# Last two tiles of tokens summed in PSUM: seeds from ScalarE, and a final norm that reads PSUM by halves

## The chip, the cores and the metric

The kernel runs on one core of a Trainium2 chip. A core has five engines, each with an instruction queue of its own: TensorE (PE in the profile, with its weight loads as PEld), VectorE (DVE), ScalarE (ACT), GpSimd (POOL) and SyncE (SP), which here issues nearly all the DMAs. PSUM, where TensorE's products land, has eight banks of 128 partitions x 512 float32 values; ScalarE and VectorE read and write it, too. The metric is the device time of one execution in microseconds (us); less is better.

## The reference, cut to what matters

One decoder layer for 512 tokens of 1024 channels: two kinds of attention, a residual, a mixture of 32 experts (each token goes to two of them), a second residual, and a last RMSNorm. What matters here is the end:

```python
x = x + hierarchical_moe(rmsnorm(x, ffn_norm[l]), ...)     # out[slot_tok] += ys * slot_w
return rmsnorm(x, final_norm)                              # x * rsqrt(mean(x*x) + eps) * final_norm
```

So the output of a token needs the sum of its residual row and of all its experts' rows, then the sum of squares over its 1024 channels, then one scaling of the row by a factor of its own and by the norm's gains.

## The kernel before, in words

The 512 tokens stand in four tiles of 128 tokens, `self.x2[0]` to `self.x2[3]`, each 128 partitions x 1024 float32 in SBUF. The experts are worked through in 16 pairs (`experts`, q = 0 to 15). A pair takes 64 slots of tokens for each of its two experts, so 128 rows. Its steps are: gate and up products into the PSUM tiles `G` and `U` (`gate_up`, L778), SiLU on ACT (L783) and a product on DVE (L784), a transposition of the result (`act_T`: L790 on PE, a copy on ACT, L792), the down products by halves of 512 channels (`down_products`, L804, tile `yp`), and a split of each half into a high and a low float32r part, scaled by the slot's weight (`down_split`: L811 on ACT, then L812 on DVE).

For most pairs the rows come back to their tokens by a product with a one-hot matrix `S` (`combine`): for each half and each of the four tiles two matmuls (high part L824, low part L825) write a PSUM tile `cp`, and VectorE adds it to `x2[t]` (L826). That makes 8 combines, 16 matmuls and 8 additions a pair. They are not done in their own pair: the list `todo` carries them into the next one, where PE takes five after the gate and up products and three after the transposition. Five pairs (`VIA`) go through DRAM instead; what they gathered is added to a tile by `take_slots` and L914, the last of it in pair 14, to `x2[3]`.

PSUM at that stage: `G` and `U` one bank each (pool `gp`), two banks for `yp` (pool `yp`, tag "y"), four for `cp` and the transpositions (pool `mp2`, tag "m").

The last pair ends in `last`. There PE computes both halves of the down products, then combines: half 0 of tile 0, and from there half 0 of the next tile and half 1 of this one in turn. As soon as a tile is whole, `final_factor` squares it with a sum on ACT (L965, which takes an instruction that reads the accumulator, and L966, which adds epsilon), `final_power` raises the sum to -1/2 on POOL (L969), and `final_scale` multiplies tile, factor and gains on DVE (L976) and issues the DMA to the output on SP (L977; tile 3 in two halves). Tile 0 goes another way: POOL multiplies it by the gains early (L946, into `o`), and ACT scales it by its factor (L952, DMA L953).

The order on PE and POOL is that of the program over all of `experts`; in `last` that holds for DVE and ACT as well. Everywhere else, and on SP always, the framework's planner sets the order by its own estimates of time. After `last` comes `overflow`: every engine loads a count (L995) and branches (L996) around a block that runs only if an expert has more than 64 tokens; the inputs here don't enter it.

Of the kernel before, what the change touches and what calls it, by code (L numbers as in the profile page):

```python
# [10 lines left out]
F32 = mybir.dt.float32  # L11
# [5 lines left out]
AF = mybir.ActivationFunctionType  # L17
ALU = mybir.AluOpType
# [3 lines left out]
P = 128  # L22
T = 512
NT = T // P
# [12 lines left out]
class Layer:  # L37
# [757 lines left out]
    def down(self, wd, aT, sw, half):  # L795
        return self.down_split(self.down_products(wd, aT, half), sw, half)

    def down_products(self, wd, aT, half):
        nc = self.nc
        yp = self.yp.tile([P, 512], F32, name="yp", tag="y")  # L800
        for j in range(2):
            for e in range(2):
                es = slice(64 * e, 64 * e + 64)
                nc.tensor.matmul(yp[es], aT[:, j, es], wd[e][:, j * D + half * 512:j * D + half * 512 + 512],  # L804
                                 start=j == 0, stop=j == 1)
        return yp
# [10 lines left out]
        self.nc.vector.tensor_scalar(S, self.tm, xf, None, ALU.is_equal)  # L817
        return S

    def combine(self, S, y, half, t):  # L820
        nc = self.nc
        hs = slice(half * 512, half * 512 + 512)
        cp = self.mp.tile([P, 512], F32, name="cp", tag="m")
        nc.tensor.matmul(cp, S[:, t * P:(t + 1) * P], y[0], start=True, stop=False)  # L824
        nc.tensor.matmul(cp, S[:, t * P:(t + 1) * P], y[1], start=False, stop=True)  # L825
        nc.vector.tensor_tensor(self.x2[t][:, hs], self.x2[t][:, hs], cp, ALU.add)  # L826

    def slot_rows(self):

# [32 lines left out]
    def experts(self):  # L862
        nc, tc = self.nc, self.tc
        NP = NE // 2
        wgu, wd = {}, {}
        for q in range(3):
            wgu[q], wd[q] = self.load_gu(q), self.load_d(q)
        self.yhl = self.wp.tile([P, 2048], F32R, name="yhl", tag="whi")
        with tc.manual_schedule(engines={mybir.EngineType.PE, mybir.EngineType.Pool}):
            xT, sw, xg = {0: self.xT0}, {}, {}  # L870
            S, y, todo, taken = None, None, [], []
            for q in range(NP):
                if q > 0 and q + 2 < NP:
                    wgu[q + 2], wd[q + 2] = self.load_gu(q + 2), self.load_d(q + 2)
                    if q + 2 == NP - 1:
                        self.load_final()
                r = wg[:, NE:NE + 1] if q else None

                def some(n):
                    for _ in range(min(n, len(todo))):  # L880
                        self.combine(S, y[todo[0][0]], *todo[0])
                        todo.pop(0)

                def between(j):
                    if q == 0 and j == 3:
                        self.tokens()
                        xg[1] = self.gather_rows(self.xi[:, 1:2], self.rows)
                    if q == 0 and j == 5:
                        sw[0] = self.take_weights()
                    if q == 0 and j == 9:  # L890
                        self.count_blocks()
                a = self.gate_up(wgu.pop(q), xT.pop(q), lambda: r if q else sw[0][1], between)
                def next_rows():
                    xT[q + 1] = self.new_xT()
                    for g in range(2):
                        self.gathered_T(xg[q + 1][0], xT[q + 1], g)
                if q == 0:
                    next_rows()
                n = min(len(todo), 4) if VIA[0] <= q <= VIA[-1] + 1 else len(todo)
                some((n + 1) // 2 + (n > 4))  # L900
                aT = self.act_T(*a)
                if q:
                    sw[q] = [self.slot_weights(q, wg, nc.scalar.copy)[:, 0:1]]
                some(n // 2 - (n > 4))
                if 0 < q < NP - 1:
                    next_rows()
                if q + 1 < NP:
                    wg = xg.pop(q + 1)[1]
                if q + 2 < NP:
                    xg[q + 2] = self.gather_rows(self.xi[:, q + 2:q + 3])  # L910
                if q == 1:
                    self.slot_rows()
                for t, r in taken:
                    nc.vector.tensor_tensor(self.x2[t], self.x2[t], r, ALU.add)  # L914
                t = q - VIA[-1] - 1
                taken = [self.take_slots(t, i) for i in range(2)] if 0 <= t < NT else []
                dn = wd.pop(q)
                if q in VIA:
                    self.down_out(dn, aT, sw[q][0], q)
                    continue  # L920
                S = self.one_hot(self.xf[:, q:q + 1])
                y = [None, None]
                todo = [(h, t) for h in range(2) for t in range(NT)]
                if q == NP - 1:
                    self.last(S, dn, aT, sw[q][0])
                    break
                for h in range(2):
                    y[h] = self.down(dn, aT, sw[q][0], h)

    def last(self, S, dn, aT, sw):  # L930

        nc, E = self.nc, mybir.EngineType
        self.out = [self.big.tile([P, 2, D], F32, name="fin", tag="big") for _ in range(2)]
        with self.tc.manual_schedule(engines={E.DVE, E.Activation}):
            nc.scalar.mul(self.fin[:, 0], self.fin[:, 0], D ** 0.5)
            yp = [self.down_products(dn, aT, h) for h in range(2)]
            y = [self.down_split(yp[0], sw, 0), None]
            self.combine(S, y[0], 0, 0)
            y[1] = self.down_split(yp[1], sw, 1)
            for t in range(NT):  # L940
                if t + 1 < NT:
                    self.combine(S, y[0], 0, t + 1)
                self.combine(S, y[1], 1, t)
                if t == 0:
                    o = self.out[0][:, 0]
                    nc.gpsimd.tensor_tensor(o, self.x2[0], self.fin[:, 0], ALU.mult)  # L946
                self.final_factor(t)
                if t:
                    self.final_power(t)
                if t == NT - 2:  # L950
                    self.final_power(0)
            nc.scalar.mul(o, o, self.rf[0])  # L952
            nc.sync.dma_start(self.io["out"][0, 0:P, :], o)  # L953
            for t in range(1, NT):
                self.final_scale(t, 2 if t == NT - 1 else 1)

    def load_final(self):
        nc = self.nc
# [92 lines left out]
    def run(self):  # L1051
        tc, ctx = self.tc, self.ctx
        self.oT = [None, None]
        self.nw, self.loads, self.rf = 0, [], {}
        PS = dict(space=PSUM, reuse_waits="tile")
        SB = dict(reuse_waits="tile")
        ctx.enter_context(tc.tile_pool(name="edge", bufs=1, side="right")).tile([P, 24], F32, name="pad")
        self.wp = ctx.enter_context(tc.tile_pool(name="wp", bufs=2, side="right", **SB))
        with ExitStack() as a:
            self.acc = a.enter_context(tc.tile_pool(name="acc", bufs=4, **PS))  # L1060
            self.mp = a.enter_context(tc.tile_pool(name="mp", bufs=3, **PS))
            self.op = a.enter_context(tc.tile_pool(name="op", bufs=1, **PS))
            with tc.tile_pool(name="rw", bufs=2, side="left", **SB) as self.rw:
                self.normed_T()
                self.load_consts()
                self.mla_compress()
                self.route_setup()
                self.mla_qkv()
                self.attention(0, range(4))
                self.moba_qkv()  # L1070
                self.attention(1, range(4))
            self.bl = ctx.enter_context(tc.tile_pool(name="bl", bufs=3, side="left", **SB))
            Ga = self.gate_T(CC + 1536)
            Gb = self.gate_T(CC + 2560)
            self.mix(Ga, Gb)
            self.attn_out()
        self.gp = ctx.enter_context(tc.tile_pool(name="gp", bufs=1, **PS))
        self.yp = ctx.enter_context(tc.tile_pool(name="yp", bufs=2, **PS))
        self.mp = ctx.enter_context(tc.tile_pool(name="mp2", bufs=4, **PS))
        self.experts()  # L1080
        self.overflow()
# [186 lines left out]
```

## Time and profile before

| | |
|---|---|
| time, median of 3 runs | 682.37 us (682.04 to 683.69) |
| the profiled execution | 683.7 us, of it span 681.9 us |
| PE busy | 661.3 us (97% of the span) |
| DVE, ACT, POOL busy | 376.1, 283.3, 83.3 us |
| chain that ended last | PE 92%, DVE 4%, ACT 1%, DMA 1% |

The span runs from the first to the last instruction that the profiler saw; the 1.8 us between span and time lie around it. L12 is line 12 of the kernel. A row of the timeline gives start, duration, engine, line, operation, the tiles (out<-in), how many, and in brackets how long the engine had been idle and what ended it. Names with a q at their end (SPq, POOLq) are an engine's sequencer: it loads registers, branches and issues DMAs.

### The profile page before, as it was taken

Reading aid. Unit: us, or ns where it says so; the run is one execution under the profiler, and the core shown is the slowest. Engines: PE = TensorE matmul, PEld = TensorE weight load, DVE = VectorE, ACT = ScalarE, POOL = GpSimd, SP = SyncE. Lnnn points to the kernel's source line nnn. Section 1 sums busy time; section 2 is a strip of 40 time slices with the busy share of each in tenths; the row PEclk is TensorE's granted clock in tenths of the full one; section 3 lists DMA queues with packets and bytes.
Section 4 is the critical chain, followed back from the end, with each engine's and each line's share of the span. In section 5 each row is a group of like instructions: output and inputs, shape, how many; then the busy total and the mean of one; then the engine's idle time right before and its main releaser. Section 6 shows DMA issues by size and latency. Waiting matters only on the chain.

```text
span 681.9 us, 11080 instructions
## 1 busy us (share of the span) xinstructions
PE 661.3 (97%) x4182; PEld 508.6 (75%) x4182; DVE 376.1 (55%) x944; ACT 283.3 (42%) x653; POOL 83.3 (12%) x127
## 2 busy tenths in 40 slices
PE   7999999999999999999999999999999999999991
PEld 7998887777788888888888899755666566666651
DVE  4624957877847983533568224643234332566654
ACT  4737545654639673433334153322222222222223
POOL 0604000000000000000000001212111111334303
PEclk8999999999999999999999999999999999999996
DMA  7733442101073026221398948799999999999953
GB/s 254 128 103 66 86 163 73 62 1 62 15 200 96 1 63 185 68 87 62 137 331 306 392 169 287 256 408 408 409 415 416 410 410 414 415 412 416 413 194 125
DMA packets 75656, 152.06 MB, mean 223 GB/s; under 512 B 31860, under 2 KB 54476, under 8 KB 63824
## 3 DMA queue, kind: packets, MB, share of 16 engines
q1 hardware_dynamic: 67616, 138.70, 55.9%
q0 software_dynamic: 4944, 8.35, 3.6%
q10 hardware_dynamic: 3040, 4.27, 2.4%
q8 instruction: 34, 0.56, 0.3%
q14 instruction: 22, 0.18, 0.1%
HBM read 149.57 MB, written 6.88 MB: 229 GB/s over the span
## 4 chain that ended last, share of the span: by engine, by line
PE 92%; DVE 4%; ACT 1%; DMA 1%; issue 1%; POOL 0%; SPq 0%; POOLq 0%; DVEq 0%
PE yp L804 8%; PE G L778 8%; PE U L778 8%; PE pacc L97 5%; PE pacc L96 5%; PE pacc L95 5%; PE pacc L451 4%; PE pacc L449 4%; PE pacc L450 4%; PE cp L824 3%; PE ptr L422 3%; PE cp L825 3%; PE S L404 3%; PE O L430 2%; PE pacc L493 2%; PE pacc L494 2%
## 5 line engine op out<-in xcount | busy, mean ns | idle before, releaser
L66 DVE SCALAR_TENSOR_TENSOR wlo<-wraw,ms,whi 128x256 fp32r<-128x256 f32 (+2 forms) x134 | 68.3, 551 | 31.1 <-ACT whi L65 30.9
L65 ACT ACTIVATE whi<-wraw,ms 128x256 fp32r<-128x256 f32 (+2 forms) x134 | 67.0, 560 | 42.1 <-PE pacc L450 19.8
L95 PE MATMUL pacc<-whi,hThi 128*128 128x352 f32 (+1 forms) x192 | 73.0, 380 | 0.0
L96 PE MATMUL pacc<-wlo,hThi 128*128 128x352 f32 (+1 forms) x192 | 70.4, 368 | 0.0
L97 PE MATMUL pacc<-whi,hTlo 128*128 128x352 f32 (+1 forms) x192 | 70.4, 366 | 0.0
L784 DVE SCALAR_TENSOR_TENSOR a<-U,wg,a 128x256 f32<-128x256 f32 x15 | 10.3, 686 | 101.8 <-issue 68.9
L804 PE MATMUL yp<-w,a 128*64 128x512 f32 x256 | 58.5, 598 | 0.5 <-ACT a L792 0.5
L778 PE MATMUL G<-w,xT 128*64 128x256 f32 x512 | 58.3, 380 | 0.0
L778 PE MATMUL U<-w,xT 128*64 128x256 f32 x512 | 58.2, 379 | 0.0
L778 PEld LDWEIGHTS G<-w,xT 128*64 128x64 f32 x512 | 36.5, 137 | 24.6 <-issue 4.9
L826 DVE TENSOR_TENSOR x<-x,cp 128x512 f32<-128x512 f32 x88 | 54.2, 682 | 0.8 <-PE cp L825 0.8
L778 PEld LDWEIGHTS U<-w,xT 128*64 128x64 f32 x512 | 36.7, 137 | 18.4
L449 PE MATMUL pacc<-hThi,whi 128*128 128x512 f32 x128 | 50.4, 393 | 0.0
L451 PE MATMUL pacc<-hThi,wlo 128*128 128x512 f32 x128 | 50.3, 393 | 0.0
L450 PE MATMUL pacc<-hTlo,whi 128*128 128x512 f32 x128 | 49.9, 390 | 0.0
L417 ACT ACTIVATE E<-E,mx 128x128 f32<-128x128 f32 (+3 forms) x64 | 35.6, 558 | 20.4 <-DVE mx L414 19.6
L1107 POOL TENSOR_SCALAR sq<-sq 128x1 f32<-128x1 f32 x4 | 0.9, 220 | 343.4 <-ACT junk L1104 343.4
L95 PEld LDWEIGHTS pacc<-whi,hThi 128*128 128x128 f32 x192 | 36.5, 190 | 4.9 <-issue 1.4
L96 PEld LDWEIGHTS pacc<-wlo,hThi 128*128 128x128 f32 x192 | 36.6, 191 | 4.2 <-issue 0.7
L804 PEld LDWEIGHTS yp<-w,a 128*64 128x64 f32 x256 | 17.0, 136 | 30.2 <-issue 27.8
L97 PEld LDWEIGHTS pacc<-whi,hTlo 128*128 128x128 f32 x192 | 36.4, 189 | 3.9 <-issue 0.2
L824 PE MATMUL cp<-yhl,S 128*128 128x512 f32 x88 | 37.6, 427 | 0.0
(232 smaller groups left out, 1338.8 us busy)
## 6 DMA issues: line engine op xcount, KB each, us to landing
w<-in_w_exp_gate_dram SPq DMA_DIRECT2D x32, 1024.0 KB
w<-in_w_exp_up_dram SPq DMA_DIRECT2D x32, 1024.0 KB
w<-in_w_exp_down_dram SPq DMA_DIRECT2D x30, 1024.0 KB
wraw<-in_w_in_dram SPq DMA_DIRECT2D x14, 1024.0 KB
wraw<-in_w_out_dram SPq DMA_DIRECT2D x4, 1024.0 KB
wraw<-in_w_in_dram SPq DMA_DIRECT2D x5, 704.0 KB
yd<-y POOLq DMA_DIRECT2D x5, 512.0 KB, 8.5
xs<-in_x_dram SPq DMA_DIRECT2D x4, 512.0 KB
```

Of the source, the lines that this page charges most:

```text
L65: nc.scalar.mul(hi[:, k], raw[:, k], g)
L66: nc.vector.scalar_tensor_tensor(lo[:, k], raw[:, k], g, hi[:, k].bitcast(F32), ALU.mult, ALU.subtract)
L95: nc.tensor.matmul(ps[t][:, :ncols], act_hi[kk // 4][:, kk % 4, ts], hi[:, k], start=kk == 0, stop=False)
L96: nc.tensor.matmul(ps[t][:, :ncols], act_hi[kk // 4][:, kk % 4, ts], lo[:, k], start=False, stop=False)
L97: nc.tensor.matmul(ps[t][:, :ncols], act_lo[kk // 4][:, kk % 4, ts], hi[:, k], start=False, stop=kk == ktot - 1)
L449: nc.tensor.matmul(ps, hi[:, k, ds], self.hT[0][k // 4][:, k % 4], start=k == 0, stop=False)
L450: nc.tensor.matmul(ps, hi[:, k, ds], self.hT[1][k // 4][:, k % 4], start=False, stop=False)
L451: nc.tensor.matmul(ps, lo[:, k, ds], self.hT[0][k // 4][:, k % 4], start=False, stop=k == KD - 1)
L778: nc.tensor.matmul(GU[i][es, 0:256], xT[:, j, es], gu[e][i][:, j * 256:(j + 1) * 256], start=j == 0, stop=j == KD - 1)
L804: nc.tensor.matmul(yp[es], aT[:, j, es], wd[e][:, j * D + half * 512:j * D + half * 512 + 512], start=j == 0, stop=j == 1)
L824: nc.tensor.matmul(cp, S[:, t * P:(t + 1) * P], y[0], start=True, stop=False)
L826: nc.vector.tensor_tensor(self.x2[t][:, hs], self.x2[t][:, hs], cp, ALU.add)
```

## The change

The last pair starts with `seed`: ScalarE copies the four halves of tiles 2 and 3 from SBUF into PSUM, tile 2 into two of the four "m" banks, tile 3 into both "y" banks. From there on `combine` for these tiles adds its two matmuls onto the seeded bank and does no VectorE addition; this holds for pair 14's products (which are combined during pair 15, in the order of tiles 0, 2, 1, 3) and for pair 15's. As the "y" banks are taken, pair 15's down products go to the two "m" banks left, and half 0 of tiles 1 and 0 in `last` to the banks of `G` and `U`.

In `last` the order becomes: half 0 of tiles 2, 3, 1, 0, then half 1 of tiles 2, 3, 1, 0. `final_part` squares half a tile straight from PSUM and adds epsilon or the first half's sum. Tiles 2 and 3 are scaled first, by halves from PSUM, and leave in one DMA each; tile 1 is scaled from SBUF in two halves; tile 0 keeps its way over POOL and ACT. POOL's order is the factors of tiles 2 and 3, the multiplication for tile 0, the factors of tiles 1 and 0. At the end ACT copies the four halves back from PSUM to `x2`, for `overflow`.

```diff
-    def down_products(self, wd, aT, half):
+    def down_products(self, wd, aT, half, at=None):
         nc = self.nc
-        yp = self.yp.tile([P, 512], F32, name="yp", tag="y")
+        pool, tag = at or (self.yp, "y")
+        yp = pool.tile([P, 512], F32, name="yp", tag=tag)
...
-    def combine(self, S, y, half, t):
+    def combine(self, S, y, half, t, at=None):
...
+        sums = self.sums.get((half, t))
+        if sums is not None:
+            for yi in y:
+                nc.tensor.matmul(sums, S[:, t * P:(t + 1) * P], yi, start=False, stop=yi is y[1], skip_group_check=True)
+            return
...
+    def seed(self):
+
+        for t, pool, tag in ((NT - 2, self.mp, "m"), (NT - 1, self.yp, "y")):
+            for h in range(2):
+                self.sums[h, t] = ps = pool.tile([P, 512], F32, name="sum", tag=tag)
+                self.nc.scalar.copy(ps, self.x2[t][:, h * 512:h * 512 + 512])
...
+                if q == NP - 1:
+                    self.seed()
+                    todo = [(h, t) for t in (0, 2, 1, 3) for h in range(2)]
...
-            yp = [self.down_products(dn, aT, h) for h in range(2)]
-            y = [self.down_split(yp[0], sw, 0), None]
-            self.combine(S, y[0], 0, 0)
-            y[1] = self.down_split(yp[1], sw, 1)
-            for t in range(NT):
-                if t + 1 < NT:
-                    self.combine(S, y[0], 0, t + 1)
+            yp = [self.down_products(dn, aT, h, (self.mp, "m")) for h in range(2)]
+            y = [self.down_split(yp[0], sw, 0)]
+            for t in (2, 3):
+                self.combine(S, y[0], 0, t)
+            y.append(self.down_split(yp[1], sw, 1))
+            for t, tag in ((1, "G"), (0, "U")):
+                self.combine(S, y[0], 0, t, (self.gp, tag))
+            for t in (2, 3):
+                self.final_part(t, 0)
+            for t in (2, 3):
                 self.combine(S, y[1], 1, t)
-                if t == 0:
-                    o = self.out[0][:, 0]
-                    nc.gpsimd.tensor_tensor(o, self.x2[0], self.fin[:, 0], ALU.mult)
+                self.final_part(t, 1)
+                self.final_power(t)
+            for t in (1, 0):
+                self.combine(S, y[1], 1, t)
                 self.final_factor(t)
-                if t:
-                    self.final_power(t)
-                if t == NT - 2:
-                    self.final_power(0)
+            for t in (2, 3):
+                for h in range(2):
+                    hs = slice(h * 512, h * 512 + 512)
+                    nc.vector.scalar_tensor_tensor(self.out[1][:, t % 2, hs], self.sums[h, t], self.rf[t], self.fin[:, 0, hs],
+                                                   ALU.mult, ALU.mult)
+                nc.sync.dma_start(self.io["out"][0, t * P:(t + 1) * P, :], self.out[1][:, t % 2])
+            o = self.out[0][:, 0]
+            nc.gpsimd.tensor_tensor(o, self.x2[0], self.fin[:, 0], ALU.mult)
+            for t in (1, 0):
+                self.final_power(t)
             nc.scalar.mul(o, o, self.rf[0])
             nc.sync.dma_start(self.io["out"][0, 0:P, :], o)
-            for t in range(1, NT):
-                self.final_scale(t, 2 if t == NT - 1 else 1)
+            self.final_scale(1, 2)
+            for (h, t), ps in self.sums.items():
+                nc.scalar.copy(self.x2[t][:, h * 512:h * 512 + 512], ps)
...
+    def final_part(self, t, h):
...
+        nc.scalar.activation(self.fin[:, 1, hs], self.sums[h, t], AF.Square, accum_out=r)
+        nc.scalar.activation(r, r, AF.Identity, bias=self.rf[t] if h else self.eps)
+        self.rf[t] = r
```

## Rows read from the trace of the kernel before

**Rows 1.** The chain of waits that ended last, from pair 15's combines on: start, duration, engine, tile and line.

```profile
655.21 0.43 PE cp L824
...
659.34 3.58 PE yp L804 x16
662.92 0.43 PE cp L824
663.36 0.25 PE cp L825
...
663.72 0.51 issue
664.24 0.75 DVE yhl L812
...
674.08 0.62 DVE fin L976
```

**Rows 2.** SP's queue at the end: the five output DMAs by the timeline (start, duration of the issue), then SP's other instructions by their lines (count, shortest/median/longest duration in ns, first and last start in us), and SP's longest wait on itself (us in total, times, longest).

```profile
671.14 0.35 SPq L977 DMA_DIRECT2D out_dram<-fin  x1
672.87 0.34 SPq L977 DMA_DIRECT2D out_dram<-fin  x1
673.26 0.42 SPq L953 DMA_DIRECT2D out_dram<-fin  x1
674.06 0.46 SPq L977 DMA_DIRECT2D out_dram<-fin  x1
674.73 1.03 SPq L977 DMA_DIRECT2D out_dram<-fin  x1
...
L995 SPq TENSOR_LOAD <-nblk x1: 1024/1024/1024, 675.8 to 675.8; - x1
L996 SPq COMPARE_BRANCH  x1: 50/50/50, 677.2 to 677.2; - x1
L996 SPq EVENT_SEMAPHORE  x8: 17/17/17, 679.6 to 680.2; - x8
SPq L996 <- SPq L996: 2.4, 1, 2.4
```

**Rows 3.** Stretches of the end: from:to, length, busy time of PE, PEld, DVE, ACT, POOL (instructions), granted TensorE clock, share of the DMA engines, GB/s.

```profile
673.75:677.75 4.00, 0.00 (x0) 0.00 (x0) 0.95 (x2) 0.00 (x0) 0.00 (x0) 0.50 0.99 386
677.75:681.90 4.15, 0.00 (x0) 0.00 (x0) 0.00 (x0) 0.00 (x0) 0.00 (x0) 0.50 0.02 4
```

**Rows 4.** ACT by the timeline, pairs 14 and 15 and `last`.

```profile
648.38 0.69 ACT L811 ACTIVATE yhl<-yp,sw 128x512 fp32r<-128x512 f32 x1 [0.99 <-PE yp L804]
651.81 0.72 ACT L783 ACTIVATE a<-G,wg 128x256 f32<-128x256 f32 x1 [2.74 <-PE G L778]
657.98 0.38 ACT L792 COPY a<-G 128x256 f32<-128x256 f32 x1 [5.45 <-PE G L790]
...
662.97 0.69 ACT L811 ACTIVATE yhl<-yp,sw 128x512 fp32r<-128x512 f32 x1 [0.97 <-PE yp L804]
666.29 1.06 ACT L965 ACTIVATE fin<-x 128x1024 f32<-128x1024 f32 x1 [2.64 <-DVE x L826]
...
667.48 0.29 ACT L966 ACTIVATE rstd<-rstd,eps 128x1 f32<-128x1 f32 x1
667.68 1.04 ACT L965 ACTIVATE fin<-x 128x1024 f32<-128x1024 f32 x1
...
672.07 1.15 ACT L952 ACTIVATE fin<-fin,rstd 128x1024 f32<-128x1024 f32 x1 [0.20 <-POOL rstd L969]
```

**Rows 5.** POOL in `last` by the timeline (the last row holds two instructions), and the same power at an earlier place, from the groups by line (count | busy, mean ns of one | idle before).

```profile
666.40 2.39 POOL L946 TENSOR_TENSOR fin<-x,fin 128x1024 f32<-128x1024 f32 x1 [29.47 <-issue]
...
670.58 0.94 POOL L969 TENSOR_TENSOR rstd<-rstd,mhalf 128x1 f32<-128x1 f32 x1 [0.79 <-ACT rstd L966]
671.50 1.75 POOL L969 TENSOR_TENSOR rstd<-rstd,mhalf 128x1 f32<-128x1 f32 x2
...
L196 POOL TENSOR_TENSOR ms<-ms,mhalf 128x1 f32<-128x1 f32 x12 | 6.8, 571 | 1.0
```

**Rows 6.** DVE by the timeline, from pair 14 to the end.

```profile
647.53 1.22 DVE L914 TENSOR_TENSOR x<-x,y 128x1024 f32<-128x1024 f32 x1
648.66 1.40 DVE L812 SCALAR_TENSOR_TENSOR yhl<-yp,sw,yhl 128x512 fp32r<-128x512 f32 x2
655.32 0.68 DVE L784 SCALAR_TENSOR_TENSOR a<-U,wg,a 128x256 f32<-128x256 f32 x1 [5.25 <-issue]
...
662.03 0.75 DVE L812 SCALAR_TENSOR_TENSOR yhl<-yp,sw,yhl 128x512 fp32r<-128x512 f32 x1 [0.85 <-ACT yhl L811]
663.63 0.69 DVE L826 TENSOR_TENSOR x<-x,cp 128x512 f32<-128x512 f32 x1 [0.85 <-PE cp L825]
...
664.90 4.36 DVE L826 TENSOR_TENSOR x<-x,cp 128x512 f32<-128x512 f32 x7
669.83 1.28 DVE L976 SCALAR_TENSOR_TENSOR fin<-x,rstd,fin 128x1024 f32<-128x1024 f32 x1 [0.58 <-POOL rstd L969]
671.56 1.28 DVE L976 SCALAR_TENSOR_TENSOR fin<-x,rstd,fin 128x1024 f32<-128x1024 f32 x1 [0.44 <-POOL rstd L969]
673.28 1.42 DVE L976 SCALAR_TENSOR_TENSOR fin<-x,rstd,fin 128x512 f32<-128x512 f32 x2 [0.44 <-POOL rstd L969]
```

**Rows 7.** Who waited for whom between 655 us and the end: us in total, times, longest.

```profile
PE cp L825 <- DVE yhl L812: 0.7, 1, 0.7
```

More of the change, by code (lines that the diff above doesn't have):

```diff
@@ L818, in one_hot @@
         return S
-    def combine(self, S, y, half, t):
+    def combine(self, S, y, half, t, at=None):
         nc = self.nc
         hs = slice(half * 512, half * 512 + 512)
-        cp = self.mp.tile([P, 512], F32, name="cp", tag="m")
+        sums = self.sums.get((half, t))
[3 more added lines that the diff above has]
+            return
+        pool, tag = at or (self.mp, "m")
+        cp = pool.tile([P, 512], F32, name="cp", tag=tag)
         nc.tensor.matmul(cp, S[:, t * P:(t + 1) * P], y[0], start=True, stop=False)
@@ L957, in load_final @@
+            self.sums = {}
+    def final_part(self, t, h):
+        nc = self.nc
+        r = self.small.tile([P, 1], F32, name="part", tag="part", bufs=4)
+        hs = slice(h * 512, h * 512 + 512)
+        nc.scalar.activation(self.fin[:, 1, hs], self.sums[h, t], AF.Square, accum_out=r)
+        nc.scalar.activation(r, r, AF.Identity, bias=self.rf[t] if h else self.eps)
+        self.rf[t] = r
     def load_final(self):
@@ L1053, in run @@
         self.oT = [None, None]
-        self.nw, self.loads, self.rf = 0, [], {}
+        self.nw, self.loads, self.rf, self.sums = 0, [], {}, {}
         PS = dict(space=PSUM, reuse_waits="tile")
```

## The prediction, made before the changed kernel ran

> **What bounds the kernel now.** I read the page's chain by engine first: PE holds 92% of it, so up to the last product of pair 15 only PE's own work counts. Then the chain in order of time from pair 15's combines on [rows 1]: PE without a gap from 655.21 to 662.92, and behind that a relay in which every engine has a turn: the first combine ends at 663.36 + 0.25 = 663.61, DVE splits the second half only at 664.24 (it adds tile 0 first), and the last scaling ends at 674.08 + 0.62 = 674.70. Then SP's queue [rows 2], because 681.9 - 674.7 = 7.2 us come after the last arithmetic. The last output DMA is issued from 674.73 to 675.76; from 675.8 SP loads the count, branches at 677.2, waits 2.4 us on nothing but itself, and from 679.6 runs through its final semaphores. The output's data are through at 677.75 [rows 3], before SP comes to look for them. So the span ends 681.9 - 675.76 = 6.14 us after SP has issued its last DMA, and what the change is worth is how much earlier that issue is done.
>
> **Up to 662.92: nothing.** PE's instructions in pair 15 stay the same in number: 16 matmuls of combines, two transpositions, 16 down products. What is new is whom they wait for. *Seeds*: four ACT copies of 128x512. The nearest row is L811, 0.69 us for that size [rows 4]; four take at most 2.8. `x2[3]` is whole at 647.53 + 1.22 = 648.75, the "y" banks are read out at 648.66 + 1.40 = 650.06 [rows 6], and ACT is idle from 649.07 to 651.81 [rows 4]: two copies up to 650.5, two up to 651.9. SiLU would start 0.1 late at most, and its result is wanted on DVE at 655.32 [rows 6]. If the planner puts the seeds behind SiLU (652.53), they end at 655.3, and PE reaches the first of them, its third combine, at 655.21 + 0.68 + 0.47 = 656.4; a late seed would hold up all that PE still has to do. Cost 0, between 0 and 1.0 (two seeds put behind L792, which ends at 658.36: until 659.8, where PE wants tile 3 from 658.41 and adds 0.47 per half). *Two "m" banks for four*: PE hands over a combine every 0.47 us, DVE adds in 0.61 ((4.36 - 0.68)/6 [rows 6]). In the new order two seeded combines stand between the second and the third that need a bank: PE asks for the first bank again at 657.3, DVE frees it at 655.9 + 0.68 = 656.6; the down products ask at 659.34, with the addition done by 658.5. Cost 0; the bound is a whole DVE instruction (0.68) for each of the six reuses. Four DVE additions fall away there beside PE's work and give nothing. The copies back at the end take ACT at most 2.8 us from 673.0 to 675.8, over 3 us before SP's final semaphores: 0.
>
> **From 662.92 on, step by step.**
> 1. PE: eight matmuls of half 0 in a row. Combines end at 663.61 and then every 0.47 us: tile 2, 3 (664.08), 1 (664.55), 0 (665.02). DVE is free, so the second split runs 663.69 to 664.44, and PE's wait of 0.7 for it [rows 7] is gone. Half 1: tiles 2 at 665.49, 3 at 665.96, 1 at 666.43, 0 at 666.90.
> 2. ACT is free at 662.97 + 0.69 = 663.66. A whole tile's sum of squares takes 1.39 from Square to Square (667.68 - 666.29 [rows 4]), later ones 1.37. Half a tile: between 0.85 (Square at half of 1.04) and 1.02 (Square as long as L811's 0.69 for that size); I take 0.95, about the middle of two close ends. Four parts start at 663.68, 664.63, 665.58 and 666.53, and PE is ahead of each. The sum stands 1.48 after a whole tile's start (667.48 + 0.29 - 666.29), so 1.05 after a half's: tile 2 at 666.63, tile 3 at 667.58. Then tile 1 from 667.48 and tile 0 from 668.85, sum at 670.33.
> 3. DVE: four additions, the last two from 666.46, done at 667.75.
> 4. POOL: a power takes 0.57 [rows 5]: tile 2 done at 667.28, tile 3 at 668.23. Then the multiplication for tile 0, 2.39 [rows 5], 668.27 to 670.66. Here it stands ahead of tile 1's factor; before, its place was idle time. Powers of tile 1 and 0: 671.25 and 671.80.
> 5. DVE scales tiles 2 and 3 from PSUM; two halves take 1.42 [rows 6], and L812, which reads PSUM, takes the same 0.75 for one: done at 669.17 and 670.5. Tile 1's halves wait for POOL: 672.03 and 672.70. ACT scales tile 0 from 671.82 to 672.97 (1.15 [rows 4]).
> 6. SP: tile 2 at 669.2, tile 3 at 670.5, tile 1 at 672.06 and 672.73, tile 0 at 673.19, done at 673.61. In the old queue the last issue took 1.03 where the others took 0.34 to 0.46 [rows 2]; it was the fourth output DMA within 1.9 us, and data of three were still ahead of it (DMA engines 0.99 busy to 677.75 [rows 3]). Now two big ones leave 3.5 and 2.2 us earlier, so I take 0.42; with 1.03 the end moves by 0.6.
>
> Sum: 675.76 - 673.61 = 2.15 us less. If the planner sends tile 0 between tile 1's halves (673.0 to 673.42, second half to 673.88), 1.9. The middle, 2.0: the profiled execution would be 683.7 - 2.0 = 681.7; against the median of the runs shown, 682.37, that is 680.4.
>
> **A rule weighed.** POOL's last two powers that met a scaling on DVE took 0.94 and about 1.23 instead of 0.57 [rows 5], and ended 0.4 after that scaling's end: 670.58 + 0.94 = 671.52 against 669.83 + 1.28 = 671.11, and 673.25 against 672.84. The one in between, which began at 671.50, just before DVE did at 671.56, was done when ACT went on with it at 672.07 [rows 4]. POOL's multiplication in contrast ended at 668.79 while DVE went on adding from PSUM to 669.26 [rows 5, 6]. The Trainium skill ("SBUF — State Buffer", section "Who interferes with whom") has a rule for this: a DVE instruction with two SBUF inputs and a GpSimd instruction that reads SBUF exclude each other, the first to start wins, and one with at most one SBUF input doesn't contend. By that rule, the trace agrees: the scalings of tiles 2 and 3 have one input in PSUM and leave POOL alone, as in my sum, and the only meeting left is tile 1's scaling with tile 0's power, the second rival below.
>
> **The rivals.**
> *A. The gain is larger than the sum*, since SP's 2.4 us after its branch ran while output data were moving [rows 2, 3], and those now end some 2 us earlier: if that shrinks by up to 1 us, 679.4. For it: no other cause for the wait is seen. Against it: the branch also comes 2 us earlier, so both stand as before to each other.
> *B. Tile 0 is later or first in line.* If DVE's scaling of tile 1 begins before tile 0's power, POOL ends 0.41 after it (673.1), ACT at 674.26, the last issue at 674.7: 1.05 less, 681.3. Against: in the old trace the power directly behind another began ahead of DVE. If SP has tile 0 first and tile 1's halves wait behind it: 673.39, 673.85, 674.31, 1.45 less, 680.9. For: that is the program's order; against: the old queue had moved tile 0 behind tiles 1 and 2.
> *C. The change doesn't bring what it says, as POOL is shut out by every DVE instruction*, those from PSUM, too. Place: the multiplication for tile 0. The power of tile 2 ends only after the additions (668.1), that of tile 3 at 668.7, and DVE runs tiles 2 and 3 to 671.5 first; the multiplication ends at 673.9, tile 1's power at 674.45, ACT's scaling at 676.2, the issue at 676.6: 0.85 more than before, 683.2; half of it, 682.3. It decides from a start of the multiplication at 670.6 on. Against: the old multiplication ran beside additions.
> *D. Slower, by the two banks.* If the planner hands out the bank that was freed last, PE waits for a whole addition at each reuse. Six times 0.68 is 4.1 us more on PE, less the 2.0: 684.5. It decides from three such waits on. For: in pair 15 nothing but DVE frees these banks. Against: the order leaves 0.7 us of air at each reuse.
>
> **How the numbers follow.** About 0.3%, or 2.05 us, is what a measurement of this kernel can tell from no change, so below 680.32 counts as faster. Forecast (1.6 to 2.4 less): 0.56, of it 0.31 below that line, since 2.15 is the sum with each step in its place and 1.9 the one with the other queue order. A: 0.08, faster. B: 0.17, no difference. C: 0.11, nearly all no difference, 0.01 slower. D: 0.08, of it 0.06 slower. So faster 0.39, same 0.54, slower 0.07. The range runs from A's 679.4 to half of C at 682.6; outside are C's upper part, D, and what lies below A. The likeliest's own range is 680.0 to 680.8.
>
> **What would show it.** In the new trace: no idle PE between 655 and 667, the last combine done at about 666.9; six sums of squares on ACT, four at a distance of 0.95; POOL's multiplication from about 668.3 for 2.4; powers of 0.6 but for one that meets tile 1's scaling; SP's last issue done at about 673.6, and 6.1 us from there to the end. Wrong it would be if PE waits in pair 15 (seeds or banks), if the multiplication takes over 3 us, or if the stretch after SP's last issue isn't of fixed length.

## The result, and the profile after

The changed kernel took 686.51 us (median of 8 runs, 685.23 to 687.41), the kernel before on the same chip 682.35 us (8 runs, 682.03 to 683.87). The ratio is 1.0052 [1.0041, 1.0064]: some 3.6 us slower, where 2.0 us faster was forecast. The profiled execution took 686.64 us with a span of 684.9 us, at a mean granted clock of 0.990 as before (0.989). Profiles differ within their first 22 us already, with the same instructions there (by then PE is 1.4 us earlier in that of e2 below than in the one before, and 1.4 later in that of e3), so traces are compared here stretch by stretch and not by their spans.

Busy time by engine, from the page:

```profile
PE 665.9 (97%) x4182; PEld 509.1 (74%) x4182; DVE 371.7 (54%) x938; ACT 288.5 (42%) x667; POOL 82.1 (12%) x127
```

PE has 4.6 us more than the 661.3 before, with its share unchanged; the work that left DVE and came to ACT (376.1 to 371.7, 283.3 to 288.5) is that of the diff. The next view is the chain of the changed kernel, from pair 15 on (start, duration, engine, tile and line). The row of G is the start of pair 15, in the rows `fin L992` ACT squares half a tile, in `part L993` it adds epsilon or the first half's sum.

```profile
652.62 3.45 PE G L778 x32
...
659.53 0.43 PE cp L831
...
660.65 0.93 PE sum L827 x4
...
663.67 3.61 PE yp L805 x16
...
667.30 0.69 ACT yhl L812
667.99 0.66 ACT fin L992 x2
...
668.67 0.29 ACT part L993
...
670.53 0.30 ACT part L993
...
670.91 0.58 POOL part L1008
...
672.33 2.35 POOL fin L977
...
675.19 0.53 POOL rstd L1008
...
675.74 0.84 ACT fin L980
```

And the one row of the same view of the kernel before that answers to the first:

```profile
648.31 3.45 PE G L778 x32
```

Two things can be read from these two views. Pair 15 starts 652.62 - 648.31 = 4.31 us later, although nothing before it was meant to change. And from the end of the last down product to the end of the span it is 684.9 - (663.67 + 3.61) = 17.62 us, where it was 681.9 - 662.92 = 18.98 [rows 1]: the end became 1.36 us shorter. 4.31 + 0.05 - 1.36 = 3.0, the difference of the two spans (0.05: the stretch from G to the last down product).

The end itself, on SP: its output DMAs by the timeline, then its other instructions by their lines, and its wait on itself, as in [rows 2].

```profile
673.38 1.66 SPq L975 DMA_DIRECT2D out_dram<-fin  x2
676.92 0.33 SPq L981 DMA_DIRECT2D out_dram<-fin  x1
677.30 1.19 SPq L1016 DMA_DIRECT2D out_dram<-fin  x2
...
L1034 SPq TENSOR_LOAD <-nblk x1: 896/896/896, 678.5 to 678.5; - x1
L1035 SPq COMPARE_BRANCH  x1: 50/50/50, 679.8 to 679.8; - x1
L1035 SPq EVENT_SEMAPHORE  x8: 17/17/17, 682.6 to 683.2; - x8
SPq L1035 <- SPq L1035: 2.8, 1, 2.8
```

Tile 0 (L981) stands ahead of tile 1's two halves (L1016). They had been scaled on DVE by 675.23 + 1.41 = 676.64, and SP sent them only behind tile 0, from 677.30 on. The other rows of the end, by the timeline, with the answers to [rows 4 to 6]: the four seeds and SiLU on ACT, POOL, and DVE.

```profile
649.04 1.11 ACT L840 COPY sum<-x 128x512 f32<-128x512 f32 x2
653.76 1.25 ACT L840 COPY sum<-x 128x512 f32<-128x512 f32 x2 [0.37 <-DVE yhl L813]
656.12 0.72 ACT L783 ACTIVATE a<-G,wg 128x256 f32<-128x256 f32 x1 [1.12 <-PE G L778]
...
671.81 0.55 POOL L1008 TENSOR_TENSOR part<-part,mhalf 128x1 f32<-128x1 f32 x1 [0.32 <-ACT part L993]
674.65 1.05 POOL L1008 TENSOR_TENSOR rstd<-rstd,mhalf 128x1 f32<-128x1 f32 x2
...
671.95 2.72 DVE L973 SCALAR_TENSOR_TENSOR fin<-sum,part,fin 128x512 f32<-128x512 f32 x4
675.23 1.41 DVE L1015 SCALAR_TENSOR_TENSOR fin<-x,rstd,fin 128x512 f32<-128x512 f32 x2 [0.56 <-POOL rstd L1008]
```

The seeds are done before SiLU, and the table of waits from 655 us on has no row in which PE waits for a seed or for a bank in pair 15.

So the loss lies ahead of the change. By the starts of the same matmuls the two profiles are level at 22 us; PE is 0.4 us behind at 183 us, 4.2 at 384, and 4.3 from 404 to pair 15. Nearly all of the loss thus builds up little by little between about 190 and 390 us: the instructions on PE and SP stand there in the order they had, without a new wait. What differs is the pace of the float32r matmuls that stream 512 columns. Two groups of them by line, in the kernel before (count, shortest/median/longest duration in ns, first and last start in us):

```profile
L449 PE MATMUL pacc<-hThi,whi x128: 387/389/490, 210.8 to 326.7; 128*128 128x512 f32 x128
...
L473 PE MATMUL pacc<-oThi,whi x64: 389/389/389, 327.4 to 370.2; 128*128 128x512 f32 x64
```

and in the changed one:

```profile
L449 PE MATMUL pacc<-hThi,whi x128: 390/393/482, 211.8 to 329.4; 128*128 128x512 f32 x128
...
L473 PE MATMUL pacc<-oThi,whi x64: 390/393/404, 330.2 to 374.1; 128*128 128x512 f32 x64
```

Durations overlap in the pipeline, so the pace is read from first and last start: L473's went from 42.8 to 43.9 us. The same 27 us of that stage in windows (from:to, length, busy time of PE, PEld, DVE, ACT, POOL with instructions, granted clock, DMA share, GB/s), before and then after:

```profile
333.00:360.00 27.00, 27.00 (x120) 22.34 (x120) 19.64 (x35) 9.28 (x20) 0.00 (x0) 1.00 0.87 296
```

```profile
336.00:363.00 27.00, 27.00 (x118) 21.89 (x117) 19.55 (x35) 9.30 (x20) 0.00 (x0) 1.00 0.83 288
```

PE is never idle in either, the clock is fully granted in both, DVE and ACT do the same work beside it: 118 matmuls where 120 went through.

### The profile page after: what moved, and what is told of

Its sections match the earlier page's. It is cut to its first block, busy times and chain, and to the rows that moved or that the text cites. A ratio compares the mean times of both kernels' runs of the same rounds, so it can differ in the third digit from the quotient of the medians.

```text
span 684.9 us, 11085 instructions
## 1 busy us (share of the span) xinstructions
PE 665.9 (97%) x4182; PEld 509.1 (74%) x4182; DVE 371.7 (54%) x938; ACT 288.5 (42%) x667; POOL 82.1 (12%) x127
## 4 chain that ended last, share of the span: by engine, by line
PE 94%; ACT 2%; DMA 1%; DVE 1%; POOL 1%; issue 0%; SPq 0%; POOLq 0%; ACTq 0%
PE yp L805 8%; PE G L778 8%; PE U L778 8%; PE pacc L96 6%; PE pacc L97 6%; PE pacc L95 6%; PE pacc L451 4%; PE pacc L449 4%; PE pacc L450 4%; PE cp L831 3%; PE ptr L422 3%; PE cp L832 3%; PE S L404 3%; PE O L430 2%; PE pacc L493 2%; PE pacc L495 2%
## 5 line engine op out<-in xcount | busy, mean ns | idle before, releaser
L449 PE MATMUL pacc<-hThi,whi 128*128 128x512 f32 x128 | 50.9, 398 | 0.0
L833 DVE TENSOR_TENSOR x<-x,cp 128x512 f32<-128x512 f32 x80 | 49.5, 683 | 1.3 <-PE cp L832 1.2
L452 DVE TENSOR_TENSOR gate<-pacc,ms 128x512 f32<-128x512 f32 x16 | 11.0, 690 | 46.4 <-PE pacc L451 46.4
```

The lines of the kernel that those rows point to most:

```text
L449: nc.tensor.matmul(ps, hi[:, k, ds], self.hT[0][k // 4][:, k % 4], start=k == 0, stop=False)
```

## The experiments

**The theories.** `final_part` gives its tiles a tag of their own, "part": four tiles of one float32 per partition, each padded to 32 bytes, so 128 bytes per partition in the pool `small`. In SBUF the big pools lie above `small`, and by the addresses in the built program the pool `big`, which holds the streamed operands, moved from byte 19072 to 19200 of each partition. The split weights (pool `wp`) lie at the other end of SBUF and stayed. Counted modulo 256 bytes, both stood at 128 before; after, the streamed tiles stand at 0. Theory 1: this shift alone is the loss. The rival: PE is slower through something else that the change brought, such as the work that the planner moved. Three kernels test it from both sides: the old kernel with 128 bytes left free in `small`, the new one without the extra tag, and the old one with 256 bytes left free.

`e1_before_128`:

```diff
         self.out = [self.big.tile([P, 2, D], F32, name="fin", tag="big") for _ in range(2)]
+        self.small.tile([P, 32], F32, name="shift", tag="shift", bufs=1)
```

> The old kernel with 128 bytes per partition left free in the pool of small tiles, as the change's four new tiles take there; nothing else differs. Theory 1 (the addresses: every SBUF tile of the large pool lies 128 bytes higher, and matmuls that stream 512 columns from there take some 5 ns longer each): 686.5 us, PE reaches the last pair's first combine 4.3 us later, all of it gained between 190 and 400 us. Theory 2 (something that the change does itself, the order of instructions or the PSUM banks): 682.4 us, no difference.

`e2_after_same_addresses`:

```diff
-        r = self.small.tile([P, 1], F32, name="part", tag="part", bufs=4)
+        r = self.small.tile([P, 1], F32, name="part", tag="rstd", bufs=4)
```

> The changed kernel with its four new small tiles in the slots that the factors of the last norm already have, so that all addresses are those of the old kernel. Theory 1: PE reaches 662.9 us as before, the end keeps the gain that the profile of the changed kernel shows behind that point (3.0 - 4.35 = -1.35): 681.0 us. Theory 2: 686.5 us, as the changed kernel.

`e3_before_256` is `e1_before_128` with 64 floats in the shift tile.

> The old kernel with 256 bytes left free in place of 128. Theory 1 with a rule of alignment to 256 bytes: 682.4 us, as without any shift. Theory 1 without such a rule (the further, the slower, or any other place than the old one): 686 us or more. Theory 2: 682.4 us, and so does not differ here from the first form of theory 1; e1 tells them apart.

Measured, medians with that of the kernel before (683.41 us) on the same chip: e1 687.75, ratio 1.0063 [1.0043, 1.0083]; e2 680.75, 0.9966 [0.9953, 0.9979]; e3 682.42, 0.9996 [0.9984, 1.0007]. Free bytes without any of the change cost what the change cost; the change without the shift gains; twice the shift costs nothing. The lines of L473 say the same, in e1 and then in e2:

```profile
L473 PE MATMUL pacc<-oThi,whi x64: 392/395/398, 330.3 to 374.4; 128*128 128x512 f32 x64
```

```profile
L473 PE MATMUL pacc<-oThi,whi x64: 389/389/389, 325.9 to 368.8; 128*128 128x512 f32 x64
```

44.1 us in e1, 42.9 in e2. Theory 1 holds, the rival falls.

**Which address counts?** The place of the streamed operand by itself, or its place against the weights? In `e4_before_128_weights_too` both move by 128 bytes, in `e9_before_weights_alone` only the weights, in `e8_before_64` the streamed operand moves by 64 (16 floats in the shift tile). The edit for the weights, which e4 adds to e1's and e9 has alone:

```diff
-        ctx.enter_context(tc.tile_pool(name="edge", bufs=1, side="right")).tile([P, 24], F32, name="pad")
+        ctx.enter_context(tc.tile_pool(name="edge", bufs=1, side="right")).tile([P, 56], F32, name="pad")
```

> The old kernel with 128 bytes left free as in e1, and the pool at the other end of SBUF, which holds the split weights, moved by 128 bytes as well. If what counts is how the streamed operand lies against the stationary weights: 682.4 us. If the place of the streamed operand alone counts: 686.5 us. Matmuls that stream the weights (the first projections) could change, too, by at most the same 5 ns each, 576 of them: 3 us more or less.

> The old kernel with 64 bytes left free. e1, e3 and e4 say that a matmul takes longer when the streamed operand lies 128 bytes off the weights, counted modulo 256, and not when it lies 0 off. At 64 bytes off: if the cost grows with the distance, 684.5 us; if only the full 128 hurts, 682.4 us; if anything but 0 hurts, 686.6 us. In matmuls with 512 columns that is 229, 227 or 232 ns from start to start.

> The old kernel with only the pool at the other end of SBUF, the split weights, moved by 128 bytes; the large pool stays where it was. If what counts is how the streamed operand lies against the weights modulo 256, this is as bad as e1 though not one streamed activation has moved: a ratio of 1.005 to 1.006 (some 4 us more), 232 ns from start to start in the gates' matmuls. If the place of the streamed operand alone counted: 1.000.

Measured: e4 682.60, 0.9993 [0.998, 1.0007]; e8 684.84 against 683.16, 1.0027 [1.0013, 1.0041]; e9 688.27 against 683.39, 1.0061 [1.0043, 1.0078]. L473 in e9:

```profile
L473 PE MATMUL pacc<-oThi,whi x64: 392/395/398, 330.6 to 374.8; 128*128 128x512 f32 x64
```

L473 takes 42.9 us from first to last start in e3, 42.8 in e4, 43.2 in e8 and 44.2 in e9, and the loss of PE up to pair 15 is 4.7 us in e1 and 5.2 in e9. So the two places count against each other: moving either by 128 costs the same by the ratios, moving both costs nothing, and by e3 the relation repeats after 256 bytes. 64 bytes cost less, 0.0027 against 0.0063 by the medians, with intervals that almost touch.

**Is it TensorE alone?** `e12_matmuls_alone`, a kernel of its own that ran once, has blocks of 64 float32r matmuls of 512 columns on zeros, and nothing beside them until its last four blocks. In blocks weighta to weighth the weights' address moves by 0, 32, ... 224 bytes, in streama to streamh that of the streamed operand; busya, busyc, busye, busyg repeat offsets 0, 64, 128 and 192 with DVE and ACT working beside them. The sizes of its tiles put streamed operand and weights at the same place modulo 256 bytes when both offsets are 0.

```diff
+            for j in range(8):
+                last = run("weight" + LET[j], 0, 8 * j)
+            for j in range(8):
+                last = run("stream" + LET[j], 8 * j, 0)
```

> Not the layer at all: it leaves the whole computation out and writes zeros. TensorE alone, 64 float32r matmuls of 128x128 by 512 columns in a block, eight weight tiles and four streamed ones in turn, all data zero. Nine blocks with the streamed tiles fixed and the weights 0, 32, 64 to 224 bytes further on, eight with the weights fixed and the streamed tiles moved instead, then four blocks (0, 64, 128, 192) during which ACT and DVE copy in SBUF. Theory a (two reads of TensorE itself, the weights' and the stream's, disturb each other): blocks at 128 take 232 ns from start to start, at 0 227, in the quiet blocks as in the busy ones. Theory b (it takes the traffic of ACT and DVE, or of DMAs): quiet blocks all alike, busy ones 227 and 232. Theory c (it takes the layer's data or access patterns): all blocks alike.

Rows of its chain (start, duration of a block, tile, line):

```profile
21.48 14.52 PE weighta L43 x64
36.00 14.93 PE weightb L43 x64
...
80.84 14.88 PE weighte L43 x64
...
110.65 14.67 PE weightg L43 x64
...
169.69 14.66 PE streamc L43 x64
...
229.20 14.94 PE streamg L43 x64
```

A block takes 14.52 us at offset 0, 14.93 at 32, 14.88 at 128, and 14.67 when the weights stand 192 bytes further on, which is where they stand when the stream is 64 further on (streamc, 14.66; the reverse, streamg, 14.94). Of the other quiet blocks streama, at offset 0, took 14.51 us, the rest 14.93 to 14.99. By 64: 226.9 ns a matmul at 0, 229 where the weights stand 192 further on, and 232 to 234 at every other offset. The case of a stream 64 bytes further on is e8's, and it has 0.14 of the 0.36 us of offset 128, some two fifths, as e8 had of e1's cost by the medians. The busy blocks have the same pace; by line:

```profile
L43 PE MATMUL busya<-m,w x64: 388/389/398, 258.9 to 273.2; 128*128 128x512 f32 x64
...
L43 PE MATMUL busyc<-m,w x64: 390/396/398, 273.4 to 288.1; 128*128 128x512 f32 x64
```

63 steps in 14.3 us are 227 ns, in 14.7 us 233. It takes no second engine, no DMA and none of the layer's data, so theories b and c fall. What is left of the three is theory a, the two reads of TensorE itself, the stream and the next weights. That they disturb each other is argued by exclusion: no run holds one of the two reads back, and which part of the chip they meet in stays open. The Trainium skill ("SBUF — State Buffer", section "Who interferes with whom") gives PE two independent read ports and has it wait for no other engine; the busy blocks agree with the second, and on the first the offsets show a loss of 1 to 3% that goes with the two addresses.

**What holds the end up?** With the shift away, 1.36 us at the end can be looked at by themselves. `e5_tile0_issued_last` is e2 with tile 0's DMA behind tile 1's, `e6_no_copies_back` is e2 without the four ACT copies, `e7_halves_on_pool` is e5 with POOL's multiplication in two halves, the first ahead of the powers of tiles 2 and 3.

```diff
-            nc.sync.dma_start(self.io["out"][0, 0:P, :], o)
             self.final_scale(1, 2)
+            nc.sync.dma_start(self.io["out"][0, 0:P, :], o)
```

> e2's kernel with one line moved: tile 0's output DMA is issued behind tile 1's two halves. In the profile of the changed kernel SP issues tile 0 at 676.92, and tile 1's halves, scaled at 675.98 and 676.64, only at 677.30 and 677.83, done at 678.48. Theory (the end hangs on when SP is done with its last issue): the halves leave at 676.0 and 676.7, tile 0 at 677.1, done at 677.5, 0.9 less: 679.8 us. Rival (the end hangs on the landing of all the data, or on another engine): 680.7 us as e2.

```diff
-            for (h, t), ps in self.sums.items():
-                nc.scalar.copy(self.x2[t][:, h * 512:h * 512 + 512], ps)
```

> e2's kernel without the four copies from PSUM back to SBUF at its end (they serve only the block for more than 64 tokens at an expert, which these inputs don't enter). Prediction's step: they lie beside SP's last issues and its wait, so 680.7 us as e2. Rival (ACT comes too late to the end): up to the copies' 2.0 us less, 678.7 us.

```diff
+            nc.gpsimd.tensor_tensor(o[:, 0:512], self.x2[0][:, 0:512], self.fin[:, 0, 0:512], ALU.mult)
             for t in (2, 3):
...
-            nc.gpsimd.tensor_tensor(o, self.x2[0], self.fin[:, 0], ALU.mult)
+            nc.gpsimd.tensor_tensor(o[:, 512:D], self.x2[0][:, 512:D], self.fin[:, 0, 512:D], ALU.mult)
```

> e5's kernel with POOL's multiplication for tile 0 cut in two: its first half runs ahead of the powers, as soon as half 0 of tile 0 is whole. Theory (POOL's 2.35 us ahead of tile 1's power are on the path to the end): the power of tile 1 comes 1.1 earlier, DVE then goes from tile 3 to tile 1 without a pause, the last issue is done 0.6 earlier than in e5: 679.2 us. Rival (DVE or ACT is as late as POOL): as e5, 679.8 us.

Measured against 683.16: e5 680.77, 0.9961 [0.9947, 0.9974]; e6 681.36, 0.9973 [0.9957, 0.9988]; e7 681.35, 0.9966 [0.9951, 0.998]. None differs from e2's 0.9966 by more than the intervals, so the times decide nothing here; what follows is read from one trace each. In e5 the end is 681.3 - (661.40 + 3.61) = 16.29 us, where e2's is 679.1 - (657.90 + 3.61) = 17.59. SP in e5, by the timeline, with the row of the last down products from its chain ahead of it in a fence of its own:

```profile
661.40 3.61 PE yp L805 x16
```

```profile
671.09 1.66 SPq L975 DMA_DIRECT2D out_dram<-fin  x2
673.74 0.99 SPq L1016 DMA_DIRECT2D out_dram<-fin  x2
674.84 0.39 SPq L982 DMA_DIRECT2D out_dram<-fin  x1
```

Tile 1's halves leave while ACT still scales tile 0, and the last issue is done at 675.23, 10.22 us after the last down product; after the change as it was it is 678.49 - 667.28 = 11.21. In e6 the end is 682.5 - (661.59 + 3.61) = 17.3 us, near e2's 17.59: the copies back were worth at most 0.3. In e7 the first half keeps POOL until 667.60, and then the two powers of tiles 2 and 3 stand behind it:

```profile
666.31 1.29 POOL L964 TENSOR_TENSOR fin<-x,fin 128x512 f32<-128x512 f32 x1 [29.66 <-ACT part L994]
667.56 1.11 POOL L1009 TENSOR_TENSOR part<-part,mhalf 128x1 f32<-128x1 f32 x2
```

Its end, from the start of the very last product, is 17.19 us, e5's by the same measure 16.94: no gain. SP's last issue was done 0.24 us sooner in e7 than in e5 by that measure (10.60 against 10.84), but the stretch behind it took 6.6 us and not 6.1. The 1.3 us of e5's trace (0.9 was expected) don't show in its median beside e2's. Some profiles show something that could hide them, without its share in the timed runs: PE waits for the weights' loads in the last pairs. By the starts of the same matmuls it loses 0.7 us there in e5, 0.6 in e7, 3.7 in e6, 0.9 in e10 below, and nothing in e2 and e11. An early PE alone is not the reason: in e5 it was 1.4 us later than in the profile before, in e2 and e11 1.4 and 1.7 us earlier. In e6, from the table of waits (us in total, times, longest):

```profile
PEld U L778 <- DMA w<-in_w_exp_up_dram: 3.0, 4, 0.9
```

**A version that keeps the tag.** `e10_after_256` is the changed kernel with 128 more bytes in `small`, so that `big` stands 256 bytes from its old place; `e11_after_256_tile0_last` adds e5's order.

```diff
         self.out = [self.big.tile([P, 2, D], F32, name="fin", tag="big") for _ in range(2)]
+        self.small.tile([P, 32], F32, name="shift", tag="shift", bufs=1)
```

> The changed kernel as it is, its own tiles in place, with another 128 bytes left free, so that the large pool lies 256 bytes higher than in the old kernel. The theory of 256 bytes: as e2, a ratio of 0.9966, PE up to the last pair as in the old kernel, and 1.35 us less behind it. If e2's gain came from its use of the old slots for the sums and not from the addresses: 1.005.

> e10's kernel with tile 0's output DMA issued behind tile 1's halves, as in e5. In e5's profile the stretch behind the last down product was 1.27 us shorter than in e2's (16.94 against 18.21), where 0.9 was expected; the times in rounds, 0.9961 and 0.9966, can't tell them apart. Theory: again 1.0 to 1.3 shorter than e10's, ratio about 0.995. Rival (the end hangs on something else, and e5's profile was chance): as e10.

Measured against 683.39: e10 682.22, 0.9980 [0.997, 0.999]; e11 680.23, 0.9960 [0.9945, 0.9976]. Adding 128 bytes to the slower kernel makes it faster than the one before. e11 has the lowest median of the three; its interval overlaps e10's, but from the start of the last down product to the end its trace has 16.93 us against 18.14 in e10, the same 1.2 to 1.3 that e5 had on e2 (16.94 against 18.21). So tile 0 sent last shortens the end in both pairs of traces. e10 gained less than e2 had; in its profile the chain leaves PE (start, duration, engine, tile):

```profile
631.29 3.43 PE G L778 x31
634.72 8.85 DMA w<-in_w_exp_gate_dram
643.63 7.40 DMA w<-in_w_exp_up_dram
651.07 3.67 PE U L778 x30
```

Weights are loaded at 395 to 418 GB/s in the stretches between 500 us and that point, with the DMA engines nearly always busy (a share of 0.99 or more), and PE waits there for them. How often that happens in the timed runs one profile can't say; that it takes the missing part of e10's gain there (0.9966 was expected, as e2 had) is likely and not shown.

## Why the prediction was wrong

**Up to 662.92: nothing. This step failed.** Its argument was that PE's instructions in pair 15 stay the same in number, and that what is new is "whom they wait for". The waits came out as it said: seeds in time, banks in time, the forecast's zero for both. But it looked for a cost only where the diff has instructions, and the cost came some 260 to 460 us earlier, by a tag that allocates 128 bytes. The term stood at 0, between 0 and 1.0; it measured +4.3 us in the profile, and e1, e2, e4 and e9 show it to be the place of the streamed tiles against the weights. No rival named it. Two rivals forecast a loss, C (683.2) and D (684.5, the two banks); D's price came nearest to the 686.5 measured, by a mechanism that didn't occur.

**From 662.92 on.** The steps up to the fifth held, with 4.31 us taken off the new times. Step 2: the sum of tile 2 at 670.83 - 4.31 = 666.52 (forecast 666.63), and half tiles at a distance of 0.92 to 0.94 (0.95). Step 4: powers of 0.58 and 0.55 (0.57), the multiplication at 672.33 - 4.31 = 668.02 for 2.35 (668.27 for 2.39). DVE's scalings from PSUM took 2.72 for four (2.84) and blocked nothing on POOL. Step 6 is where 0.6 of the sum's 2.15 went. SP has tile 0 first, which was rival B's second case: it forecast the last issue done at 674.31, and it was 678.49 - 4.31 = 674.18. That is 1.58 less than 675.76. Then the stretch behind it wasn't 6.14 but 684.9 - 678.49 = 6.4, with SP's wait on itself at 2.8 instead of 2.4: another 0.3 back, which is within what that stretch varies by among the profiles here (6.0 to 6.6). 1.3 is left of 2.15, the 1.36 of the two traces within rounding. That this stretch would not be of fixed length is the one of the prediction's signs of being wrong that came. Two slips bear on nothing: tile 3's scaling would be done at 669.17 + 1.42 = 670.59 and not 670.5, and half of C stands once as 682.3 and once as 682.6, where half of 0.85 more gives 682.8.

**The rivals.** A fell: the wait behind the branch grew. B's second case came true in the end's order, with 1.45 less forecast there. C fell, the multiplication was where the forecast had it, and so did D: PE never waited for a bank.

**The forecast for the change without the shift.** e2 is that kernel: 2.3 us less than before by its ratio (0.9966 of 682.4; 1.4 to 3.2 by the interval), with 1.4 in its trace. The forecast of 2.0 lies inside. That the medians come so close to it is in part luck: the trace, which leaves out what differs ahead of the end, shows 1.4, mainly since tile 0 went ahead of tile 1. What turned the sign is thus one term, forecast 0 and measured +4.3.

## What to carry to other kernels

Read what a diff allocates as closely as what it issues: a new tag of 16 bytes' worth of data moved every pool above it, and a stage some 300 us ahead of the edit paid for it. When matmuls of a stage that wasn't touched go slower with the same order, clock and neighbours, compare first and last start of the same line in both traces, and then the operands' addresses; a free tile of 64 to 256 bytes tests it. Where a kernel's loads keep the DMA engines busy all the time, a gain read from one trace has to be timed before it is counted.

## What the hardware showed that was not expected

In `e12`, on TensorE alone, a float32r matmul of 512 columns with 128x128 weights takes 226.9 ns when the streamed operand and the weights start at the same place modulo 256 bytes of a partition, 229 when the weights stand 192 further on, and 232 to 234 at 32, 64, 96, 128, 160 and 224. In the layer L449 and L473 follow that. The combines don't, though they are float32r matmuls of the same shape: before, `S` and the split rows `yhl` start at the same place modulo 256, and nine of their matmuls, from the first row to the second, take 2.09 us, 232 ns each:

```profile
655.64 0.23 PE cp L825
...
657.73 0.22 PE G L790 x2
```

After, where they stand 128 apart, four take 0.93 us (sum L827), 232 ns again. So the same place is not enough for the quick pace; what holds the combines back stays open. Matmuls in plain float32 (the down products, 214.5 ns, and the experts' of 256 columns, 108 ns) and float32r ones of 256 and 352 columns (120 and 161 ns) kept their pace under the same shift.

SP's wait on itself behind its branch is not of fixed length: 2.4 us before [rows 2], 2.8 after, 2.9 in e7, and with these three the stretch behind the last issue goes from 6.1 to 6.4 and 6.6 us. Not always: e5 and e11 waited 2.65 us and have a stretch of 6.1.
